# Strassen operands from normalized rows, and six pools in the down stage, in a one-core hybrid encoder layer

## The chip, the cores and the metric

The kernel runs on one core of one Trainium2 chip. The metric is device time in microseconds (us), median of several runs. Engines go by their short names in the profile: PE is TensorE, DVE VectorE, ACT ScalarE, POOL GpSimd, SP SyncE (here it only starts DMAs).

## The reference, cut to what matters

One encoder layer (DEPTH is 1) is applied to two sequences of 512 rows with 1024 columns each, all in float32:

```
h = _rmsnorm(x, norm_mix_g[l])
...
x = x + (g_a * y_a + g_b * y_b) @ w_out[l]
h = _rmsnorm(x, norm_ffn_g[l])
gt, up = jnp.split(h @ w_gu[l], 2, axis=-1)
x = x + (jax.nn.silu(gt) * up) @ w_down[l]
...
return _rmsnorm(x, final_norm_g)
```

y_a is a bidirectional RWKV7 branch, y_b an attention branch. The change is in the last part: the norm ahead of the feed-forward, the product with w_gu (1024 x 5632) and the product with w_down (2816 x 1024). `_rmsnorm` divides each row by the root of its mean square and multiplies each column by a gain.

## The kernel before, in words

**Precision.** A float32 operand is split into two rounded parts, `hi` (a cast on ACT) and `lo = x - hi` (a subtraction on DVE or POOL). One product is three matmuls: hi x hi, hi x lo, lo x hi (`mm3`, L139). `split` (L135) makes the pair; all matmuls are recorded at L129, all transposes at L133 (`tr4`, four 128 x 128 blocks into one PSUM bank).

**Stages.** First the branches (to about 900 us), then `combine` of each sequence (products with w_oab, tile `pab`), the projections with w_out (`pwo`, added to the residual rows `x2`), then the feed-forward and the final norm.

**Strassen.** The feed-forward treats the two sequences together: seven block products instead of eight. With the normalized, transposed rows of sequence 0 in column halves B11 and B21 and those of sequence 1 in B12 and B22, the operands are B11, B21, B22, T1 = B12 - B11, T2 = B22 - T1, T3 = B22 - B12 and T4 = B21 - T2, each as hi and lo, of 128 x 4 x 512. B12 itself isn't kept. The weights get the matching sums S1 to S4, formed on POOL per block of 128 feed-forward columns (`a_blocks`, L1332).

**First norms** (`first_norm`, L1280): called for the four tiles of sequence 0 from inside `combine` of sequence 1, at steps 0, 2, 4 and 6 of its eight. Squares on ACT, a power on POOL, a row scaling on DVE (L1292), per half a group of four transposes (`nt_f0`), a column scaling by the gain from PSUM on DVE (L1296), the cast on ACT and the `lo` part on POOL (`EF`).

**The planned window** (L1423 to L1550). `Window` is a small planner: operations with an engine, a cost, a rank and dependences; it writes their order out ahead, and the instructions of each engine are kept in that order. It holds the last quarter of the projections (`w_project`), the norms of sequence 1 (`w_norm`), T1 to T4 (`w_norm` forms T1, B22, T2 and T3, `w_combos` T4 and the splits into memory that is free only once the projection's weights are gone, `reopen`), and the first four products of the feed-forward (`w_product`, blocks 0 and 1 with B11 and B21). There the rows of sequence 1 are scaled (L1462), transposed (two groups per tile), scaled by the gain (L1471), and everything else works on transposed data: T1 takes two subtractions (L1479, L1481), the others one or two, on POOL or DVE as the strings ET1 to ET4 and EB22 say.

**Feed-forward, first half** (`gate_up`, L1368): 22 blocks; `pgA`, `pgB` and `pgC` are its PSUM tiles. Weights come in as `graw` and `uraw` of 512 KB through three buffers (`raw`, NRAW). Results go to DRAM (`a_d`).

**Down stage** (from L1574): again seven products, over eleven pairs of blocks, two at a time (`turns`). Once the operands' pools are closed (`tp_` for T2 to T4, `evst` for the evaluation tiles, `bst` for B11, B21, B22, T1 and the products kept), one pool `fp` takes all tiles: ten halves `rh` of loaded data, eleven each of `w12`, `t` and `s` that stay resident, seven pairs of split blocks `d`, and the tiles of the ends. `p5_(0)` copies W12 from the raw tile of block 0 (L1665) and forms the first T from that copy (L1671).

All these DMAs are issued by SP, whose queue is served in order: a load that waits for its buffer holds those behind it.

Of the kernel before, what the change touches and what calls it, by code (L numbers as in the profile page):

```python
# [18 lines left out]
P = 128  # L19
# [56 lines left out]
ET2 = 'gggg'  # L76
# [3 lines left out]
C0 = 14  # L80
HK = (0, 2, 4, 6)
# [13 lines left out]
EB22 = 'gggg'  # L95
ET1 = 'ggvv'
ET3 = 'gggg'
ET4 = 'vggg'
ES = 'gg'
EF = 'gggg'  # L100
# [8 lines left out]
def trunk(ctx, tc, outs, x, w_in, w2, g2, w_uq, w_ukk, w_ukv, w_oab, w_out, w_gu, w_down,  # L109
          cols, fng, ident, te, to, mask2, reset, blk64, blk2):  # L110
# [1167 lines left out]
    B11, B21 = (operand(bp0, n) for n in ("B11", "B21"))  # L1278

    def first_norm(cp_, t):  # L1280
# [10 lines left out]
        for g, dst in enumerate((B11, B21)):  # L1291
            nc.vector.tensor_scalar_mul(h[g], xs[:, g], ss[:, 0:1])  # L1292
# [131 lines left out]
    COST = {nc.vector: ("V", 0.6), nc.gpsimd: ("G", 1.23)}  # L1424
    early, psb = {}, []

    def w_split(dst, t, src, rank, eng, *deps):
        ts = slice(t * P, (t + 1) * P)
        hi = W.op("A", 0.52, rank, lambda: nc.scalar.copy(dst()[0][:, :, ts], src()), *deps)
        lo = W.op(*COST[eng], rank, lambda: eng.tensor_sub(dst()[1][:, :, ts], src(), dst()[0][:, :, ts]), hi)  # L1430
        return hi, lo

    def w_project(t):
# [3 lines left out]
        def mms(k0):  # L1437
            if k0 == 0:
                z["ps"] = bank(1 + t % 2, f"pwo1{t}")
# [4 lines left out]
        o = psb[-4:-3]  # L1444
# [5 lines left out]
    def w_norm(t, old):  # L1450

        ts, xt, z = slice(t * P, (t + 1) * P), x2[4 + t], {}

        def square():
            z["ss"] = np_.tile([P, 1], F32, tag="nss", bufs=4, name=f"nssf1{t}")
            z["ht"] = np_.tile([P, D], F32, tag="nh", bufs=1, name=f"nhf1{t}")
            return nc.scalar.activation(z["ht"], xt, AF.Square, accum_out=z["ss"])
        o = W.op("A", 1.04, 0, square, *psb[-1:], *old.get("tr", ()))
        o = W.op("V", 0.07, 0, lambda: nc.vector.tensor_scalar(z["ss"], z["ss"], 1.0 / D, RMS_EPS,
                                                               op0=ALU.mult, op1=ALU.add), o)  # L1460
        o = W.op("G", 0.46, 0, lambda: nc.gpsimd.tensor_tensor(z["ss"], z["ss"], mhalf[:, :1], op=ALU.pow), o)
        o = W.op("V", 0.66, 0, lambda: nc.vector.tensor_scalar_mul(z["ht"], xt, z["ss"]), o)  # L1462
        r = {"tr": [], "nsc": [], "z": z}

        def tr(g):
            z["ps", g] = bank(3, f"nt_f1{t}{g}")
            tr4(z["ps", g], lambda i: z["ht"][:, (g * 4 + i) * P:(g * 4 + i + 1) * P])

        def scale(g):
            z[g] = np_.tile([P, KH, P], F32, tag=f"nsc{g}", bufs=(4, 1)[g], name=f"nscf1{t}{g}")  # L1470
            return nc.vector.tensor_mul(z[g], z["ps", g].rearrange("p (k t) -> p k t", k=KH),  # L1471
                                        cc(C_GFFN + g * KH, KH).unsqueeze(2).to_broadcast([P, KH, P]))
        for g in range(2):
            r["tr"].append(W.op("T", 0.43, 0, lambda g=g: tr(g), o, *old.get("nsc", [])[g:g + 1]))
            r["nsc"].append(W.op("V", 0.6, 0, lambda g=g: scale(g), r["tr"][g], *(old.get("b22", ()) if g else ())))
# [31 lines left out]
    def w_product(i):  # L1507
# [20 lines left out]
        for k in range(KH):  # L1528
            o = [W.op("T", 0.64, 3 + i, lambda k=k: mms(k), *o)]
# [321 lines left out]
```

## Time and profile before

| What | us |
|---|---|
| median of 3 runs | 1795.2 (1794.31 to 1796.43) |
| the profiled execution | 1793.97 |
| its span, first to last instruction | 1792.2 |
| PE busy | 1700.9 (95%) |
| DVE busy | 1075.6 (60%) |
| ACT busy | 787.9 (44%) |
| POOL busy | 627.3 (35%) |

The mean granted TensorE clock is 0.984. A row of the profile gives a line of the kernel, an engine, an operation and `out<-in` by the program's tile names with numbers left out; `x` is a count. In the table by stage each engine's busy time is followed by its number of instructions; PEclk is the granted clock as a share of full speed. Matmuls overlap in the pipeline, so one of them is reported longer (389 ns) than the step from one to the next, and a busy PE is not PE at its peak.

### The profile page before, as it was taken

The page shows a single profiled execution, that of the slowest core. Times are in us where ns is not written, and L with a number is a line of the kernel's source. Part 1 is how long each engine was busy: PE and PEld are TensorE (multiplying, and loading weights), DVE is VectorE, ACT ScalarE, POOL GpSimd, SP SyncE. Part 2 cuts the span into 40 slices and gives each one's busy share as a digit, 9 for nine tenths or more (in the row PEclk, how much of TensorE's full clock was granted, in tenths as well). Part 3 has the DMA queues.
Part 4 walks back from the last instruction along what each step waited for, and adds up shares of the span by engine and source line. Part 5 has one row for each costly group of instructions (what it writes and reads, how often), then busy time and mean ns, then how long its engine had stood idle before and what let it go on. Part 6 is the DMA issues. An engine that isn't in the chain of part 4 may idle for free.

```text
span 1792.2 us, 30028 instructions
## 1 busy us (share of the span) xinstructions
PE 1700.9 (95%) x11276; PEld 1327.8 (74%) x11276; DVE 1075.6 (60%) x1773; ACT 787.9 (44%) x1533; POOL 627.3 (35%) x984
## 2 busy tenths in 40 slices
PE   7999999999999997999999999699999999989997
PEld 6778766777777775666667877488888888868886
DVE  6734464636445365855566665955565465498657
ACT  6643424344433335666663432433333333245445
POOL 1121536274554736261012143833343333200006
PEclk9999999999999998999999999899999999999999
DMA  5473342434334344211267531123222222383442
GB/s 179 135 259 100 107 116 79 132 86 125 114 85 121 84 116 118 73 40 34 110 207 266 176 126 36 36 88 107 94 93 96 83 90 76 100 307 110 130 134 94
DMA packets 181233, 208.90 MB, mean 117 GB/s; under 512 B 102816, under 2 KB 106272, under 8 KB 181088
## 3 DMA queue, kind: packets, MB, share of 16 engines
q1 hardware_dynamic: 180224, 205.48, 36.3%
q8 instruction: 88, 1.44, 0.3%
q10 hardware_dynamic: 720, 0.98, 0.2%
q0 software_dynamic: 144, 0.52, 0.1%
q14 instruction: 57, 0.47, 0.1%
HBM read 147.70 MB, written 59.24 MB: 115 GB/s over the span
## 4 chain that ended last, share of the span: by engine, by line
PE 72%; DVE 9%; POOL 6%; DMA 6%; issue 3%; ACT 2%; SPq 1%; DVEq 0%; POOLq 0%; ACTq 0%
PE pgC L129 10%; PE pj_gt L129 8%; PE pgB L129 6%; PE pgA L129 6%; PE pj_rkv L129 4%; PE dx L129 4%; PE pwo L129 4%; PE pab L129 3%; PE s L129 2%; PE dy L129 2%; POOL el L966 2%; POOL lt L964 2%; PE sc L129 2%; PE pj_mla L129 2%; PE pav L129 2%
## 5 line engine op out<-in xcount | busy, mean ns | idle before, releaser
L964 POOL TENSOR_TENSOR lt<-lane,el 128x126 f32<-128x126 f32 (+22 forms) x248 | 94.1, 379 | 36.7 <-DMA lane<-nt_d 18.1
L966 POOL TENSOR_TENSOR el<-el,lt 128x126 f32<-128x126 f32 (+22 forms) x248 | 98.9, 399 | 19.0
L129 PE MATMUL pab<-yo,wab 128*128 128x512 f32 x384 | 96.5, 403 | 5.5 <-DVE wab L137 2.8
L129 PE MATMUL pj_gt<-h_hi,wlo_gt 128*128 128x512 f32 x240 | 98.4, 410 | 1.2 <-DVE wlo_gt L137 1.2
L129 PE MATMUL pj_gt<-h_lo,whi_gt 128*128 128x512 f32 x240 | 99.4, 414 | 0.0
L129 PE MATMUL pj_gt<-h_hi,whi_gt 128*128 128x512 f32 x240 | 99.0, 412 | 0.0
L129 PEld LDWEIGHTS pab<-yo,wab 128*128 128x128 f32 x384 | 71.7, 191 | 24.2 <-DVE wab L137 5.1
L1344 POOL TENSOR_TENSOR s<-uraw 128x512 f32<-128x512 f32 x22 | 29.3, 1334 | 154.3 <-DMA uraw<-in_w_gu 154.0
L129 PE MATMUL pwo<-woh,m 128*128 128x512 f32 x256 | 80.4, 390 | 0.0
L129 PE MATMUL pj_rkv<-h_hi,wlo_rkv 128*128 128x512 f32 x192 | 79.1, 412 | 0.0
L129 PE MATMUL pj_rkv<-h_hi,whi_rkv 128*128 128x512 f32 x192 | 78.6, 410 | 0.0
L129 PE MATMUL pj_rkv<-h_lo,whi_rkv 128*128 128x512 f32 x192 | 78.2, 407 | 0.0
L1720 POOL TENSOR_TENSOR x<-x,dp 128x512 f32<-128x512 f32 x4 | 6.3, 1593 | 177.5 <-DVE x L1719 177.5
L1412 DVE TENSOR_TENSOR p<-p,pgC 128x512 f32<-128x512 f32 x22 | 15.1, 687 | 82.3 <-PE pgC L129 82.3
L1053 ACT COPY sva<-s 64x128 f32<-64x128 f32 x64 | 16.5, 258 | 100.8 <-PE s L129 87.3
L129 PEld LDWEIGHTS pwo<-woh,m 128*128 128x128 f32 x256 | 48.1, 188 | 10.0
L1054 DVE COPY svb<-s 64x128 f32<-64x128 f32 x64 | 18.9, 295 | 60.5 <-ACT sva L1053 35.8
L775 DVE TENSOR_REDUCE mx<-sc 128x1 f32<-128x512 f32 x64 | 43.6, 687 | 15.7 <-PE sc L129 14.9
L129 PEld LDWEIGHTS pj_gt<-h_hi,wlo_gt 128*128 128x128 f32 x240 | 45.1, 188 | 9.9 <-DVE wlo_gt L137 1.7
L129 PEld LDWEIGHTS pj_gt<-h_hi,whi_gt 128*128 128x128 f32 x240 | 45.1, 188 | 8.9
L129 PEld LDWEIGHTS pj_gt<-h_lo,whi_gt 128*128 128x128 f32 x240 | 45.1, 188 | 8.6
L1354 POOL TENSOR_TENSOR s<-graw,uraw 128x512 f32<-128x512 f32 x22 | 29.2, 1325 | 63.8 <-DVE S_2l L137 5.0
(1563 smaller groups left out, 5458.4 us busy)
## 6 DMA issues: line engine op xcount, KB each, us to landing
graw<-in_w_gu SPq DMA_DIRECT2D x22, 512.0 KB, 3.6
uraw<-in_w_gu SPq DMA_DIRECT2D x22, 512.0 KB, 3.6
a_d<-a SPq DMA_DIRECT2D x21, 512.0 KB, 3.4
w<-in_w_down SPq DMA_DIRECT2D x42, 256.0 KB, 4.5
x<-in_x SPq DMA_DIRECT2D x16, 512.0 KB, 7.1
rwkv_in<-lut SPq DMA_DIRECT2D x32, 256.0 KB, 2.4
gate_d<-gtt SPq DMA_DIRECT2D x32, 256.0 KB, 2.4
wab<-in_w_oab SPq DMA_DIRECT2D x32, 256.0 KB, 3.8
```

The lines of the kernel that those rows point to most:

```text
L129: pin(nc.tensor.matmul(out, lhsT, rhs, start=start, stop=stop, **kw), n if out.shape[0] > 64 else n / 2)
L775: nc.vector.tensor_reduce(mx, sc, axis=AX.X, op=ALU.min)
L964: eng.tensor_mul(lv, lane[:, s, s + 1:].unsqueeze(1).to_broadcast([P, m_, n]), el[:, 0:m_, s].unsqueeze(2).to_broadcast([P, m_, n]))
L966: eng.tensor_add(ev, ev, lv)
L1053: nc.scalar.copy(sva[HA, :, c], s2[HA])
L1054: nc.vector.tensor_copy(svb[HB, :, c], s2[HB])
L1344: vg(ES[min(j, 1)]).tensor_add(s1, a21, a22)
L1354: vg(ES[min(j, 1)]).tensor_sub(s3, a11, a21)
L1412: nc.vector.tensor_add(p1, p1, x_)
L1720: nc.gpsimd.tensor_add(xs(1, t, 1), xs(1, t, 1), p5[t])
```

## The change

In `first_norm` the gain is multiplied into the rows before they are transposed: it comes as a tile `gain` of 128 x 1024 (`ffg`, the gain repeated on all partitions) that takes one of the three `raw` buffers. The normalized rows go to DRAM as well (`n0_d`, eight stores of 256 KB). The split reads PSUM directly, its `lo` part on DVE.

In the window, the rows of sequence 1 get the gain in the same way; the rows of sequence 0 are fetched again (`w_row`); T1, T3, T2 and T4 are formed on rows, on DVE, with one subtraction each; and T1, B22, T2, T3 and T4 are each transposed (`w_tr`: five groups of four per tile) and split from PSUM, `hi` on ACT and `lo` on DVE. The strings that put work on POOL go away. The projections of the window use one PSUM bank pair instead of two; ranks and costs of the planner are new (R1, R2, RW, RP).

In the down stage `fp` becomes six pools: `frh` (the `rh` halves), `fs`, `ft`, `fp` (ends), `fd` (split blocks) and `fw12`. The first copy of W12 moves to POOL, and the first T reads the raw tile.

```diff
@@ first_norm
         for g, dst in enumerate((B11, B21)):
-            nc.vector.tensor_scalar_mul(h[g], xs[:, g], ss[:, 0:1])
+            nc.vector.scalar_tensor_tensor(out=h[g], in0=xs[:, g], scalar=ss[:, 0:1], in1=gain[:, g * S:(g + 1) * S],
+                                           op0=ALU.mult, op1=ALU.mult)
+            nc.sync.dma_start(n0_d[t][:, g], h[g])
             ps = dn(f"nt_f0{t}{g}")
             tr4(ps, lambda i: h[g][:, i * P:(i + 1) * P])
-            sc = ld(f"nscf0{g}").rearrange("p (k t) -> p k t", k=KH)
-            nc.vector.tensor_mul(sc, ps.rearrange("p (k t) -> p k t", k=KH),
-                                 cc(C_GFFN + g * KH, KH).unsqueeze(2).to_broadcast([P, KH, P]))
-            split(dst[0][:, :, ts], dst[1][:, :, ts], sc, vg(EF[t]))
+            split(dst[0][:, :, ts], dst[1][:, :, ts], ps.rearrange("p (k t) -> p k t", k=KH))
@@ the window
+    def w_tr(t, name, i, src, dst, rank, late, *deps):
...
+        def tr():
+            z["ps"] = bank(i, f"nt_{name}{t}")
+            tr4(z["ps"], lambda c: src()[:, c * P:(c + 1) * P])
+            z["v"] = z["ps"].rearrange("p (k t) -> p k t", k=KH)
+        o = W.op("T", 0.44, rank, tr, *deps, *late, *[r[0] for r in trs[i][-1:]], *[r[1] for r in trs[i][-2:-1]])
+        hi = W.op("A", 0.6, rank, lambda: nc.scalar.copy(dst()[0][:, :, ts], z["v"]), o)
+        lo = W.op("V", 0.68, rank, lambda: nc.vector.tensor_sub(dst()[1][:, :, ts], z["v"], dst()[0][:, :, ts]), hi)
...
+    def w_row(t, g, rank, *deps):
...
+            z["w"] = np_.tile([P, S], F32, tag="w", bufs=2, name=f"n0{t}{g}")
+            return nc.sync.dma_start(z["w"], n0_d[t][:, g])
...
+        na = W.op("V", 0.7, 0, lambda: scale(0), o)
+        w, ld = w_row(t, 0, 0)
+        t1 = W.op("V", 0.7, 0, lambda: nc.vector.tensor_sub(w["w"], z["n"][:, 0], w["w"]), na, ld)
+        o1, _ = w_tr(t, "T1", 3, lambda: w["w"], lambda: T1, 0, (), t1)
+        nb = W.op("V", 0.7, R1[0], lambda: scale(1), o)
+        b22, _ = w_tr(t, "B22", 2, lambda: z["n"][:, 1], lambda: B22, R1[1], (), nb)
+        t3 = W.op("V", 0.7, R1[2], lambda: nc.vector.tensor_sub(z["n"][:, 0], z["n"][:, 1], z["n"][:, 0]), nb, t1)
+        t2 = W.op("V", 0.7, R1[2], lambda: nc.vector.tensor_sub(z["n"][:, 1], z["n"][:, 1], w["w"]), t3, b22, o1)
...
+    def w_third(t, z, t3, t2):
+        w_tr(t, "T3", 2, lambda: z["n"][:, 0], lambda: T3, R2[1] + t, (opened,), t3)
+        w, ld = w_row(t, 1, R2[2])
+        o = W.op("V", 0.7, R2[2] + t, lambda: nc.vector.tensor_sub(w["w"], w["w"], z["n"][:, 1]), ld, t2)
+        wbuf.append(w_tr(t, "T4", 3, lambda: w["w"], lambda: T4, R2[2] + t, (opened,), o)[0])
@@ the down stage
-    fp = pool(p4, "fp")
+    frh, fs, ft, fp, fd, fw12 = (pool(p4, n) for n in ("frh", "fs", "ft", "fp", "fd", "fw12"))
...
         if p == 0:
-            nc.vector.tensor_copy(W12[p], pre["draw"][0][:, hihalf])
+            nc.gpsimd.tensor_copy(W12[p], pre["draw"][0][:, hihalf])
...
-        nc.vector.tensor_sub(T_[p], W12[p], w11)
+        nc.vector.tensor_sub(T_[p], W12[p] if p else pre["draw"][0][:, hihalf], w11)
```

More of the change, by code (lines that the diff above doesn't have):

```diff
@@ L80 @@
 C0 = 14
+R1, R2, RW, RP = (1, 1, 2), (3, 10, 14), 1, 3
 HK = (0, 2, 4, 6)
@@ L1278, in trunk @@
     B11, B21 = (operand(bp0, n) for n in ("B11", "B21"))
+    n0_d = [dram.tile([P, 2, S], F32, name=f"n0_d{t}") for t in range(4)]
+    gain = fwr[0].tile([P, D], F32, tag="raw", bufs=NRAW, name="ffg")
+    nc.sync.dma_start(gain, ffg)
     def first_norm(cp_, t):
@@ L1438, in mms @@
             if k0 == 0:
-                z["ps"] = bank(1 + t % 2, f"pwo1{t}")
+                z["ps"] = bank(1, f"pwo1{t}")
             hi, lo = wo1[k0 // 2]
@@ L1448, in w_project @@
         return o[0]
[L1450 to L1459, printed above, removed]
-                                                               op0=ALU.mult, op1=ALU.add), o)
[L1461 to L1467, printed above, removed]
-        def scale(g):
[L1470 to L1475, printed above, removed]
-        def t1():
-            z["t1"] = np_.tile([P, KH, P], F32, tag="nt", bufs=3, name=f"ntf{t}")
-            return nc.vector.tensor_sub(z["t1"], z[0], B11[0][:, :, ts])
-        a = W.op("V", 0.6, 0, t1, r["nsc"][0], *(n[-3].get("T4", ()) if t > 2 else ()))
-        o = W.op("V", 0.6, 0, lambda: nc.vector.tensor_sub(z["t1"], z["t1"], B11[1][:, :, ts]), a)
-        r["T1"] = w_split(lambda: T1, t, lambda: z["t1"], 0, vg(ET1[t]), o)
-        b = w_split(lambda: B22, t, lambda: z[1], PRIOW, vg(EB22[t]), r["nsc"][1])
-        eng = vg(ET3[t])
-        d = W.op(*COST[eng], PRIOW, lambda: eng.tensor_sub(z[0], z[1], z[0]), r["nsc"][1], a)
-        eng2 = vg(ET2[t])
-        r["T2"] = W.op(*COST[eng2], PRIOW, lambda: eng2.tensor_sub(z["t1"], z[1], z["t1"]), *r["T1"], r["nsc"][1])
-        r["b22"], r["T3"] = (*b, d, r["T2"]), d
-        return r
@@ L1491, in w_combos @@
[L1491 to L1498 removed]
+    trs = {2: [], 3: []}
@@ L1535, in w_product @@
             copied.append(W.op("A", 0.48, 1, copy, *o, *copied[-1:]))
-    n, last, copied = [{}], [], []
+    n, last, copied = [], [], []
     fw = T2 = T3 = T4 = None
@@ L1541, in trunk @@
         last.append(w_project(t))
-        if t == 3:
-            opened = W.op(None, 0, 0, reopen, *last)
-            for i in range(3):
-                w_combos(i, n[i + 1])
-        n.append(w_norm(t, n[-1]))
-    w_combos(3, n[4])
+        n.append(w_norm(t))
+    opened = W.op(None, 0, 0, reopen, *last)
+    for f in (w_second, w_third):
+        for t in range(4):
+            f(t, *n[t])
     for i in range(2 * NE):
@@ L1582, in d_half, with resident @@
     def d_half(src, name):
-        raw = fp.tile([P, 512], F32, tag="rh", bufs=NRH, name=name)
+        raw = frh.tile([P, 512], F32, tag="rh", bufs=NRH, name=name)
         nc.sync.dma_start(raw, src)
         return raw
-    def resident(tag, name):
-        return fp.tile([P, 512], F32, tag=tag, bufs=JP, name=name)
+    def resident(pl, name):
+        return pl.tile([P, 512], F32, tag="r", bufs=JP, name=name)
     def d_block(src, name):
         cnt[0] += 1
-        pl, tag, bufs = (fw, "b", NBLK) if cnt[0] % 2 else (fp, "d", DBLK)
+        pl, tag, bufs = (fw, "b", NBLK) if cnt[0] % 2 else (fd, "d", DBLK)
         hi = pl.tile([P, 512], F32R, tag=f"{tag}hi", bufs=bufs, name=f"{name}h")
@@ L1813, in layout @@
     r["fng"] = np.broadcast_to(a["final_norm_g"], (P, D)).copy()
+    r["ffg"] = np.broadcast_to(a["norm_ffn_g"][0], (P, D)).copy()
     r["ident"] = np.eye(P, dtype=f)
```

60 lines of the change are left out of this document (33 added, 27 removed).

## Prediction

> **What bounds the kernel now.** I read the page's head first, then a table by stage (busy time per engine between chosen times), because the share of TensorE is an average over stages with different limits.
>
> ```profile
> span 1792.2 us, 30028 instructions
> ```
> ```profile
> core 0: us, PE busy (x) PEld busy (x) DVE busy (x) ACT busy (x) POOL busy (x), PEclk, DMA share, GB/s
> 1017.00:1063.50 46.50, 43.03 (x192) 33.97 (x192) 38.48 (x59) 20.81 (x43) 22.05 (x18) 0.96 0.42 136
> 1093.10:1117.60 24.50, 22.60 (x107) 18.28 (x105) 14.26 (x21) 7.47 (x13) 11.17 (x10) 1.00 0.00 0
> 1093.10:1167.20 74.10, 55.90 (x237) 44.13 (x236) 57.08 (x61) 28.42 (x51) 51.66 (x36) 0.88 0.07 22
> 1200.00:1550.00 350.00, 350.00 (x1546) 289.82 (x1545) 196.78 (x247) 118.96 (x203) 128.45 (x91) 1.00 0.28 91
> 1558.80:1612.60 53.80, 44.98 (x194) 35.59 (x192) 45.64 (x75) 19.75 (x35) 0.77 (x1) 1.00 0.71 254
> 1612.60:1770.00 157.40, 157.36 (x694) 130.31 (x695) 117.29 (x181) 79.22 (x148) 22.28 (x16) 1.00 0.36 111
> ```
>
> The row 1200 to 1550 is TensorE without a gap: 350 / 1546 = 0.226 us from one matmul to the next. That is the yardstick. The row after 1612 is dense too (0.227), so whatever is won before it moves the end by as much. The other rows are where the change acts, and each loses time:
> - first norms (1017 to 1063.5): 32 of the 192 are transposes, which cost 0.45 per four (row below). 160 x 0.226 + 8 x 0.45 = 39.8, so 6.7 of 46.5 is lost.
> - the planned window (1093.1 to 1167.2; last projection, second norms, Strassen operands, first products): 205 x 0.226 + 8 x 0.45 = 49.9, so 24.2 of 74.1 is lost.
> - start of the down stage (1558.8 to 1612.6): 194 x 0.226 = 43.8, so 10.0 of 53.8 is lost.
>
> Next, who makes TensorE wait in the window (the view of waits), and the groups of that stretch (the view of lines):
>
> ```profile
> PE nt_f L133 <- DVE nhf L1462: 6.6, 3, 4.7
> PE pgB L129 <- ACT T L1429: 5.9, 1, 5.9
> PE pgB L129 <- DVE T L1430: 3.7, 1, 3.7
> ```
> ```profile
> L1430 DVE TENSOR_TENSOR T<-ntf,T 128x512 fp32r<-128x512 f32 x10 | 13.1, 1330 | 0.0
> L1485 POOL TENSOR_TENSOR nscf<-nscf,nscf 128x512 f32<-128x512 f32 x4 | 6.9, 1735 | 6.3 <-ACT B L1429 3.9 <-DVE ntf L1479 2.3
> L1462 DVE TENSOR_SCALAR nhf<-x,nssf 128x1024 f32<-128x1024 f32 x4 | 6.0, 1510 | 4.8 <-POOL nssf L1461 4.8
> L1471 DVE TENSOR_TENSOR nscf<-nt_f,col 128x512 f32<-128x512 f32 x8 | 5.2, 683 | 2.1 <-PE nt_f L133 2.1
> L129 PE MATMUL pgB<-T,S_0h 128*128 128x512 f32 x8 | 4.3, 607 | 9.6 <-ACT T L1429 5.9 <-DVE T L1430 3.7
> L1344 POOL TENSOR_TENSOR s<-uraw 128x512 f32<-128x512 f32 x3 | 4.8, 1599 | 1.1 <-DMA uraw<-in_w_gu 0.8 <-PE pwo L129 0.3
> L1447 DVE TENSOR_TENSOR x<-x,pwo 128x512 f32<-128x512 f32 x4 | 2.7, 679 | 2.9 <-PE pwo L129 2.9
> ```
>
> Compare two rows of one shape: a VectorE operation takes 683 ns when one operand lies in PSUM (L1471; 679 in L1447), and 1330 ns on average when all its operands lie in SBUF (L1430), in a stretch in which GpSimd is busy 51.66 of 74.1. So VectorE and GpSimd are the bound of this stretch, partly by holding each other up; the waits named give 16.2 of the 24.2, and the rest is a slow clock after them (granted 0.88; 607 ns for a matmul of pgB).
>
> **Part 1, the window.** *Removed:* all operand work of GpSimd (the splits of B22, the differences T3 and T2, two splits of T1 and three tiles' T4: 20 operations, at up to 1.735 us, the L1485 row), and on VectorE the whole-row scaling (L1462), two column scalings and the second subtraction of T1. *Added:* differences are formed on normalized rows, so five things per tile are transposed instead of two: 12 more groups of four transposes.
>
> ```profile
> 1102.81 0.45 PE nt_f L133 x4
> ```
>
> 12 x 0.45 = 5.4 more on TensorE, all of it on the path, since the stretch is to become TensorE's. VectorE per tile: the projection's add, two scalings by row and gain, T1, T3, T2, the T4 difference and five splits, so 12 operations; 48 x 0.68 = 32.6. Nine more splits of weight blocks: 6.1. Together 38.7. It can start with the first add, 24 x 0.226 = 5.4 after 1093.1, and end at 1137.2. TensorE has 96 projection matmuls, 20 groups of transposes and 48 early products: 144 x 0.226 + 20 x 0.45 = 41.5, to 1134.6. So the two are nearly level and VectorE is 2.6 behind. GpSimd keeps about seven sums of weight blocks (L1344 and its neighbours); each can hold a VectorE operation for 1.60 - 0.68 = 0.92 if both its operands are in SBUF, 6.4 at most. The five splits now read PSUM, which the 683 ns row shows undisturbed. What is last, T4 (8 of the 48 operations), is used only four products, 48 x 0.226 = 10.8 us, later. So the loss that stays lies between 0 and 2.6 + 6.4 = 9.0, and I take 6, nearer the upper end since the order is fixed ahead and every slip stops TensorE in order. **Gain 24.2 - 5.4 - 6 = 12.8**, from 9.8 to 18.8 by these bounds.
>
> A new wait comes with it. The gain's tile takes one of the three `raw` buffers until the last row scaling, so the second half of block 0 (`uraw0`), long in memory before, is loaded after that.
>
> ```profile
> uraw<-in_w_gu SPq DMA_DIRECT2D x22, 512.0 KB, 3.6
> w<-in_w_down SPq DMA_DIRECT2D x42, 256.0 KB, 4.5
> rwkv_in<-lut SPq DMA_DIRECT2D x32, 256.0 KB, 2.4
> ```
>
> The last projection ends at 1093.1 + 96 x 0.226 + 6 x 0.45 = 1117.5; add, squares, power, two scalings behind it I put at 5 us (estimate: some seven steps of 0.68). Load from 1122.5 to 1126.1, one sum of 1.60, and a split of 2 x 0.68: S1 at 1129, before TensorE is through with its 41.5. So it costs nothing while those 1134.6 cover it, and shows in full past them. Rows of the first half are stored and fetched again (256 KB, 2.4 to 4.5 us each, eight out and eight in); the fetch for T1 has no producer nearby and is hidden, the one for T4 waits for a free buffer but has 10.8 us. Projections now use one bank pair instead of two: each is freed by a 0.68 add, two tiles (10.8 us) before it is wanted again; nothing.
>
> **Part 2, first norms.**
>
> ```profile
> 1042.84 2.75 DVE L1292 TENSOR_SCALAR nhf<-x,nssf 128x512 f32<-128x512 f32 x2
> ```
> ```profile
> 1042.61 2.69 POOL L137 TENSOR_TENSOR B<-nscf,B 128x512 fp32r<-128x512 f32 x2
> ```
> ```profile
> 1046.84 4.60 PE L129 MATMUL pab<-yo,wab 128*128 128x512 f32 x12 [2.57 <-DVE wab L137]
> ```
> ```profile
> 1038.61 3.53 DMA g<-gate_d
> ```
>
> One of the losses is seen whole here: two row scalings (2.75 us) stand as long as GpSimd splits B (2.69), the weight split behind them is late, TensorE waits 2.57. The change takes these eight GpSimd splits away, drops eight column scalings on VectorE (8 x 0.68) and puts eight splits there instead, which is level; the row scaling takes the gain with it, at 0.68 each. Two at 0.68 against 2.75 leave 1.4 per tile. Against it: SyncE now also issues eight stores of 256 KB, each of which waits for its scaled rows, and the loads of gates and weights behind them wait too (one such load, 3.53, is on the chain of waits already). Bounds: +5 (all losses but 1.7 gone) to -7 (two loads made late); I take a **gain of 2**.
>
> **Part 3, start of the down stage.** The chain of waits, and SyncE's own waits:
>
> ```profile
> 1553.62 2.72 PE pgB L129 x12
> ...
> 1562.68 2.73 PE pgC L129 x12
> ...
> 1566.16 0.69 DVE a L1413
> 1566.85 0.35 DVE w L1665
> ...
> 1567.23 0.70 DVE T L1671
> ...
> 1568.01 0.32 SPq L1323
> ```
> ```profile
> SPq L1323 <- DVE T L1671: 13.4, 1, 13.4
> ```
> ```profile
> PE dy L129 <- ACT dS_0h L136: 3.5, 1, 3.5
> ```
>
> Nothing of the pool `fp` is done on VectorE until the last use of the feed-forward's evaluation tiles (L1413); then W12's copy and the first difference T. The load of the third `araw` waits 13.4 us for that difference, and every load behind it in SyncE's queue with it; then the DMA share jumps to 0.71 over the stretch while TensorE starves. Operand memory itself falls free in turn: B11 and B21 before B22 and T1, those before the evaluation tiles, T4 last at 1562.68 + 2.73 = 1565.4. Six pools in that order let `rh`, S and T start once B22's products are done (1553.62 + 2.72 = 1556.3), nine us earlier, and the first T no longer waits for W12's copy. W12 goes to the memory that is freed last: its first load from 1565.4 lands at 1569.9, the difference and split take 3 x 0.68, 1572.0. TensorE has eight matmuls of its first products left behind T4's, to 1567.2, and two products of 12 x 0.226 before it needs them, at 1572.6. Just enough. The copy on GpSimd hides (first use a phase later), but holds one `raw` buffer some 1.5 us longer (estimate from 1.60 for a sum of that shape). The split of T for the first product needs T4's memory too: 2 x 0.68 after 1565.4, at about 1566.8. I take 2.5 of the 10.0 as staying: **gain 7.5**, bounds 0 and 10.
>
> **Sum.** 12.8 + 2 + 7.5 = 22.3. The profiled execution took 1793.97 (span 1792.2 and 1.8 around it); 1793.97 - 22.3 = 1771.7. The median of the runs is 1.2 above that execution, so 1773 against 1795.2.
>
> **Rivals.**
> - *The pools change nothing* (VectorE's order is fixed by something other than memory, or W12's late loads stop SyncE's queue as the third `araw` did). For: W12 is now on the latest memory. Against: 13.4 us for one load that needs only T. 1773 + 7.5 = 1780.5.
> - *`uraw0` comes late.* If its issue stands in SyncE's queue behind the T4 fetches, which wait for T4 transposes at about 1140 (estimate: VectorE's 1137.2 and a few slips), S1 is ready at 1140 + 3.6 + 1.6 + 1.4 = 1146.6 instead of being hidden to 1134.6; other products can't go ahead, as they all need that load. 12 more, of which 2 lie in my 6: 1773 + 10 = 1783.
> - *The clock falls.* In this row transposes follow an idle stretch and the clock is slow after it:
>
> ```profile
> 1127.49 1.94 PE L133 MATMUL nt_f<-idn,nhf 128*128 128x128 f32 x8 [4.68 <-DVE nhf L1462]
> ```
>
> After 1117.5 TensorE has 14 groups of transposes and 48 matmuls, with VectorE pacing; at half speed these 17.2 us cost 17 more: 1790. Against it: 1093.1 to 1117.6 holds 24 transposes at a granted 1.00, though between projections. The Trainium skill, "TensorE: Matmul & The Clock Gate", Part 4: PE-mode transpose, says that a transpose "doesn't count as PE-busy the same way", which speaks against this change; no stretch of transposes alone is in this trace to test it.
> - *Slower: SyncE's queue in the first norms.* Eight stores wait for their scalings ahead of loads that feed the products at once. One late load costs one landing, 3.53. If more than six of eight do (22.3 / 3.53), all is lost; with all eight, 28.2 - 22.3 = 5.9 slower: 1801. Against it: one such wait is seen in the stretch today, and there are four tiles spread over eight steps.
> - *All waits vanish:* 6 + 2.5 + 3 more gained: 1761.5.
>
> **Chances.** Forecast 0.52 (its own range 1766 to 1780), pools without effect 0.13, late `uraw0` 0.14, clock 0.07, stores 0.10, all vanish 0.04. About 0.2% (3.6 us) is what a measurement of this kernel can tell from no change; the clock's 1790 lies 1.6 beyond that, so half of its chance goes to no change. Faster 0.86, same 0.04, slower 0.10. The range 1763 to 1788 takes in the forecast, the late load, the pools, and parts of the others: 0.84.
>
> **What would show it.** Right: between the last projection and the feed-forward's first products GpSimd has only weight sums and powers; T's VectorE splits take near 0.68; no wait of TensorE in the window above 3 us; five transposed things per tile; the third `araw` load issued before 1565 less the gain so far; dy's first product right behind dx. Wrong: TensorE waiting for S1's split with GpSimd's sum waiting for `uraw` (late load), a granted clock under 0.9 after the projections with TensorE busy (clock), pab waiting for wab or g with SyncE waiting for the scaled rows (stores), or SyncE waiting for T4's last product with loads for `rh` behind it (pools).

## The result, and the profile after

The changed kernel takes 1775.63 us (median of 4 runs, 1774.83 to 1783.75), the kernel before 1795.82, measured beside it (4 runs): a ratio of 0.9897 with a 95% interval of 0.9867 to 0.9928, 13 to 24 us less. A second series with more runs gave 1775.44 against 1792.49, ratio 0.9902 (0.9884 to 0.9920). The profiled execution took 1774.83 us (span 1773.0). The forecast was 1773.0, with a range of 1763 to 1788.

The first view is the table by stage of the changed kernel; its rows stand against those of the prediction (line numbers of the changed kernel are about five lower up to `first_norm` and eight to ten higher in the down stage). Columns: stretch, its length, then each engine's busy time with its instructions, granted clock, DMA share, GB/s.

```profile
1014.00:1060.00 46.00, 44.90 (x208) 35.69 (x208) 34.19 (x62) 21.77 (x44) 12.31 (x10) 1.00 0.58 189
1089.00:1160.00 71.00, 69.05 (x339) 55.88 (x338) 55.72 (x84) 32.85 (x64) 22.43 (x18) 1.00 0.19 60
1200.00:1530.00 330.00, 330.00 (x1458) 273.25 (x1457) 184.22 (x232) 112.56 (x192) 120.02 (x86) 1.00 0.27 91
1540.00:1600.00 60.00, 56.69 (x237) 45.06 (x236) 54.63 (x90) 23.88 (x42) 1.49 (x2) 0.97 0.70 243
1600.00:1750.00 150.00, 150.00 (x647) 121.62 (x646) 107.76 (x165) 74.30 (x140) 21.88 (x16) 1.00 0.33 107
```

Read with the prediction's prices (0.226 a matmul, 0.45 for four transposes):
- First norms: 208 less 32 transposes are 176 x 0.226 + 8 x 0.45 = 43.4, so 2.6 of 46.0 is lost, against 6.7 before: 4.1 gained.
- Window: 259 x 0.226 + 20 x 0.45 = 67.5, so 3.5 of 71.0 is lost, against 24.2. Less the 5.4 for twelve more groups of transposes, 15.3 is gained. The granted clock is 1.00 and GpSimd is busy 22.43 of 71 in place of 51.66 of 74.
- Gate and up stage: 330 / 1458 = 0.2263, as before.
- The last row is the surprise: no gap, clock 1.00, and yet 150 / 647 = 0.2318 a matmul, where the kernel before had 157.4 / 694 = 0.2268. (The step from the start of one matmul to the start of the next is called the pitch from here on.)

Two rows of the window carry its mechanism: VectorE's splits from PSUM take 681 ns each, where the splits of T took 1330 on average before (L1430 there), and the longest wait of TensorE that is left is 0.9 us, where it was 5.9.

```profile
L1452 DVE TENSOR_TENSOR T<-nt_T,T 128x512 fp32r<-128x512 f32 x16 | 10.5, 681 | 0.3 <-ACT T L1451 0.2
```
```profile
PE pgB L124 <- ACT S_1h L131: 0.9, 1, 0.9
```

The timeline of TensorE shows where the time went in total: the first matmul of the `pwo` stage, the first of the down stage and the last one, in the changed kernel and then in the kernel before.

```profile
973.72 0.39 PE L124 MATMUL pwo<-woh,m 128*128 128x512 f32 x1
...
1539.88 0.39 PE L124 MATMUL dx<-P1drawh,P1arawh 128*128 128x512 f32 x1
...
1764.68 0.40 PE L124 MATMUL dx<-dT_10h,dA_10l 128*128 128x512 f32 x1
```
```profile
973.52 0.39 PE L129 MATMUL pwo<-woh,m 128*128 128x512 f32 x1
...
1558.89 0.39 PE L129 MATMUL dx<-P1drawh,P1arawh 128*128 128x512 f32 x1
...
1783.97 0.39 PE L129 MATMUL dx<-dT_10h,dA_10l 128*128 128x512 f32 x1
```

Up to the down stage 585.4 became 566.2, which is 19.2 less. The down stage itself, of which the prediction hoped for 7.5, takes 224.8 after 225.1. Its start did become better: the first S begins just before the first down product, the copy of W12 stands on GpSimd, and of four larger waits (3.5 us for `dS_0h`, which the prediction shows, and the three of the first view) one is left (the second view). After them the timelines of DVE, POOL and SP and the chain of waits, all of the changed kernel:

```profile
PE dx L129 <- ACT dA_4h L136: 2.3, 1, 2.3
PE dx L129 <- ACT dA_3h L136: 1.5, 1, 1.5
PE dy L129 <- DVE dT_1l L137: 1.1, 1, 1.1
```
```profile
PE dx L124 <- ACT dA_3h L131: 2.7, 1, 2.7
```
```profile
1539.68 0.69 DVE L1678 TENSOR_TENSOR S<-araw,a 128x512 f32<-128x512 f32 x1 [1.63 <-DMA a<-a_d]
1540.29 1.10 DVE L1679 TENSOR_TENSOR T<-draw 128x512 f32<-128x512 f32 x1
```
```profile
1540.11 0.73 POOL L1673 COPY w<-draw 128x512 f32<-128x512 f32 x1 [8.71 <-PE pgC L124]
```
```profile
1545.78 0.32 SPq L1320 DMA_DIRECT2D araw<-a_d  x1
1546.19 2.28 SPq L1675 DMA_DIRECT2D w<-in_w_down  x5
1548.58 0.36 SPq L1320 DMA_DIRECT2D araw<-a_d  x1
...
```
```profile
1548.58 8.10 DMA araw<-a_d
...
1556.78 0.63 ACT dA_3h L131
...
1557.45 2.08 PE dx L124 x4
1559.53 2.51 PE dy L124 x8
```

The load that the prediction watched, the third `araw`, goes out at 1545.78, before the first dy product. The next one goes out 2.8 us later, behind five loads of W12 on the same queue, and takes 8.10 us, in which the DMA engines are busy 0.95 of the time; TensorE waits 2.7 for it and then runs slow (four matmuls in 2.08, eight in 2.51, at a granted clock of 0.66 from 1557 to 1562). By the row 1540 to 1600, 237 x 0.226 = 53.6, so 6.4 of 60 is lost against 10.0: 3.6 gained. The slower pitch behind it gives as much back: some 700 matmuls from 1600 on at 0.005 more are 3.5.

### The profile page after: what moved, and what is told of

The parts are those of the page before. It is cut to its first block, busy times and chain, and to the rows that moved or that the text cites. A ratio compares the mean times of both kernels' runs of the same rounds, so it can differ in the third digit from the quotient of the medians.

```text
span 1773.0 us, 30134 instructions
## 1 busy us (share of the span) xinstructions
PE 1705.7 (96%) x11324; PEld 1329.0 (75%) x11324; DVE 1060.9 (60%) x1784; ACT 787.8 (44%) x1541; POOL 584.8 (33%) x957
## 4 chain that ended last, share of the span: by engine, by line
PE 71%; DMA 8%; POOL 7%; DVE 7%; issue 3%; ACT 3%; SPq 1%; DVEq 0%; POOLq 0%; ACTq 0%
PE pgC L124 10%; PE pj_gt L124 8%; PE pgB L124 7%; PE pgA L124 6%; PE dx L124 5%; PE pwo L124 4%; PE dy L124 3%; PE pj_rkv L124 3%; PE s L124 3%; POOL el L961 2%; POOL lt L959 2%; PE pab L124 2%; PE sc L124 2%; PE pav L124 2%; PE pj_mla L124 2%
## 5 line engine op out<-in xcount | busy, mean ns | idle before, releaser
L770 DVE TENSOR_REDUCE mx<-sc 128x1 f32<-128x512 f32 x64 | 43.7, 687 | 15.6 <-PE sc L124 14.8
L1177 POOL TENSOR_TENSOR g<-g 128x512 f32<-128x512 f32 x16 | 24.9, 1555 | 84.7 <-DVE g L1175 66.7
```

The costliest lines, as they stand in the source:

```text
L770: nc.vector.tensor_reduce(mx, sc, axis=AX.X, op=ALU.min)
L1177: nc.gpsimd.tensor_add(g_[:, 0], g_[:, 0], g_[:, 1])
```

## The experiments

The question is what made the same matmuls slower, then what the parts are worth, and what the two new waits cost. My first theory came from the layout of the built program. A matmul has a stationary operand (128 x 128), which is loaded ahead of it (PEld in the profile), and a moving one (128 x 512). In the down stage, its first product apart, the moving operand lies in `fd` (`fp` before) and the stationary one in `fw`. `fw` starts at byte 190,432 of each partition, 224 modulo 256 (the remainder after division by 256). So did the moving blocks before (138,464). In the changed kernel `fd` starts at 134,496, 96 modulo 256, because pool `fp` now lies below it and ends in two small tiles, `fss` and `frs`, 128 bytes together. In the gate and up stage everything starts at 224.

Two spans stand beside each median: from the first `pwo` matmul to the first down matmul (up), and from there to the last down matmul (down), both from the profiled execution; then the matmuls in the 45 us from 1640 to 1685.

| run | median us | ratio to before (95%) | up | down | matmuls |
|---|---|---|---|---|---|
| before | 1795.82 | | 585.4 | 225.1 | 200 |
| after | 1775.63 | 0.9897 (0.9867, 0.9928) | 566.2 | 224.8 | 195 |
| after_again | 1775.44 | 0.9902 (0.9884, 0.9920) | 566.3 | 224.9 | 195 |
| a_align224 | 1769.19 | 0.9870 (0.9848, 0.9892) | 566.4 | 221.0 | 200 |
| b_shift128 | 1797.87 | 1.0028 (1.0016, 1.0040) | 585.8 | 230.4 | 194 |
| early_only | 1776.98 | 0.9914 (0.9883, 0.9944) | 566.8 | 228.5 | 200 |
| down_only | 1794.13 | 0.9997 (0.9985, 1.0010) | 585.7 | 226.2 | 195 |
| one_pool | 1773.53 | 0.9889 (0.9860, 0.9918) | 565.9 | 224.0 | 200 |
| no_gain | 1772.67 | 0.9881 (0.9861, 0.9901) | 567.7 | 221.5 | 200 |
| no_stores | 1769.41 | 0.9866 (0.9844, 0.9888) | 564.8 | 222.8 | 200 |
| araw_far | 1768.51 | 0.9859 (0.9837, 0.9881) | 566.4 | 219.3 | 200 |
| best | 1768.41 | 0.9863 (0.9842, 0.9885) | 567.9 | 218.1 | 200 |
| m_offsets, one run | 1781.59 | | 575.6 | 221.7 | 196 |
| m_fine, one run | 1780.53 | | 566.6 | 225.8 | 197 |

The experiments were made in four series, and each ratio is against the kernel before of its own series: 1792.86 (`a_align224`, `b_shift128`, `early_only`, `down_only`), 1793.23 (`m_offsets`, `no_gain`, `no_stores`, `araw_far`), 1793.55 (`m_fine`, `one_pool`) and 1792.49 (`best`, `after_again`). The last series ran on another chip than the first three. Where kernels share the up part its span agrees within 0.9 us (565.9 to 566.8); the medians scatter more, since the stages ahead of `pwo` alone moved its start between 968.0 and 978.1.

### Does the place of the small tiles set the pitch?

`a_align224` changes only this in the changed kernel:

```diff
-    frh, fs, ft, fp, fd, fw12 = (pool(p4, n) for n in ("frh", "fs", "ft", "fp", "fd", "fw12"))
+    frh, fs, ft, fp, fd, fw12, fsm = (pool(p4, n) for n in ("frh", "fs", "ft", "fp", "fd", "fw12", "fsm"))
...
-        ss = fp.tile([P, 2], F32, tag="fss", ...
-        rs = fp.tile([P, 1], F32, tag="frs", ...
+        ss = fsm.tile([P, 2], F32, tag="fss", ...
+        rs = fsm.tile([P, 1], F32, tag="frs", ...
```

> The changed kernel with the two small tiles of the last norms (fss and frs, 2 x 64 B a partition) in a pool of their own behind the last one, so that the down stage's moving operands, the fd blocks, start 128 B lower: at 224 modulo 256 bytes, as the kernel before has them and as every operand of the gate and up stage lies, in place of 96 modulo 256. Nothing else moves. Theory (the start address of the moving operand sets the pitch of the matmuls): the down stage goes back from 0.232 to 0.225-0.227 us a matmul between 1600 and 1750, and the time falls by 3.5 to 5 us against the changed kernel, to about 1771 us. Rival (the slower pitch comes from the pools' other traffic, from the loads that land earlier or from the weights' tiles): the pitch stays at 0.232 and the time at 1775.

`b_shift128` does the reverse to the kernel before, in `p5_`:

```diff
         S_[p] = resident("s", f"S{p}")
+        if p == 0:
+            pad = fp.tile([P, 32], F32, tag="pad", bufs=1, name="pad")
+            nc.gpsimd.memset(pad, 0.0)
```

> The kernel before with a pad of 128 B (one tile, cleared once by GpSimd) put ahead of the moving operands of the down stage in its one pool: they start at 96 modulo 256 in place of 224, and nothing else of the change is in it. Theory (start address): the pitch of the down stage rises from 0.2245-0.2265 to 0.232 us a matmul and the time by 3.5 to 5 us, to 1799-1801 us. Rival (pools, loads): pitch and time stay, 1796 us.

The same 45 us of the down stage by stage table: first the changed kernel, then `a_align224`, then `b_shift128`.

```profile
1640.00:1685.00 45.00, 45.00 (x195) 36.49 (x194) 29.84 (x48) 19.27 (x35) 0.00 (x0) 1.00 0.39 124
```
```profile
1640.00:1685.00 45.00, 45.00 (x200) 37.28 (x199) 30.98 (x50) 19.62 (x36) 0.00 (x0) 1.00 0.41 129
```
```profile
1640.00:1685.00 45.00, 45.00 (x194) 36.21 (x193) 30.71 (x50) 19.17 (x34) 0.00 (x0) 1.00 0.32 102
```

In all three TensorE has no gap and the granted clock is 1.00; 195, 200 and 194 matmuls fit. 128 bytes ahead of the moving blocks make the whole difference, in both directions. The down stage falls by 3.8 us in `a_align224` and rises by 5.3 in `b_shift128`. The start of the stage differs in its waits and, for `b_shift128`, in its granted clock (0.91 over the first 60 us), so the fair stretch lies behind it: from the first matmul of `dy<-dT_7h,dS_7h` to the last of the stage, at a clock of 1.00 in all four, the kernel before takes 169.4 us, `a_align224` 170.0, and the changed kernel and `b_shift128` 173.4 each. So the address is worth 3.4 to 4.0 us there. The medians agree less sharply: `b_shift128` is 5.0 above the kernel before of its series; `a_align224` is 23.7 below its own, the changed kernel 20.2 and 17.1 in its two series. The rival, that loads or pools slow the matmuls, is out: `b_shift128` has neither.

### The address alone, or where the two operands stand to each other?

`m_offsets` gives every buffer of both operands a start address of its own (`d_block`; the stationary blocks likewise through a helper with five buffers):

```diff
-        hi = pl.tile([P, 512], F32R, tag=f"{tag}hi", bufs=bufs, name=f"{name}h")
-        lo = pl.tile([P, 512], F32R, tag=f"{tag}lo", bufs=bufs, name=f"{name}l")
...
+            i = (cnt[0] // 2 - 1) % DBLK
+            hi = fd.tile([P, 512], F32R, tag=f"dhi{i}", bufs=1, name=f"{name}{'abcdefg'[i]}h")
+            lo = fd.tile([P, 520 if i != 5 else 528], F32R, tag=f"dlo{i}", bufs=1, ...)
+            lo = lo[:, :512]
```

> The changed kernel, small tiles in a pool of their own, with the buffers of the down stage's matmul operands placed at different start addresses: the seven pairs of moving blocks at 224, 0, 32, 64, 96, 128 and 192 modulo 256 bytes, the five pairs of stationary blocks (also those of the gate and up stage) at 224, 0, 32, 64 and 96. The pitch of each block's twelve matmuls is read from the timeline by buffer. Theory (the moving operand's own start address counts): 0.227 us for moving blocks at 224 whatever the stationary block, 0.233 at 96, and another value for each class of the other five; the gate and up stage, where all moving operands stand at 224, keeps 0.2264 for all five stationary offsets. Rival (what counts is where moving and stationary operand stand to each other): the pitch goes with the difference of the two offsets, a moving block at 224 slows down beside a stationary one at 96, and the gate and up stage slows down for some of its five.

The letters in the names tell the buffers. The timeline below has the first and last matmul of two neighbouring blocks of twelve: `gl`/`yl` has the moving block at 192 and the stationary one at 96, `al`/`ul` has both at 224.

```profile
1635.91 0.40 PE L124 MATMUL dx<-dT_4gh,dS_4yh 128*128 128x512 f32 x1
...
1638.49 0.39 PE L124 MATMUL dx<-dT_4gh,dS_4yl 128*128 128x512 f32 x1
1638.72 0.40 PE L124 MATMUL dy<-dB_3ah,dS_3uh 128*128 128x512 f32 x1
...
1641.22 0.40 PE L124 MATMUL dy<-dB_3ah,dS_3ul 128*128 128x512 f32 x1
```

2.58 / 11 = 0.2345 in the one and 2.50 / 11 = 0.2273 in the other, side by side. The mean step in ns between starts within a block, over the whole down stage (some twenty steps each, from times printed to 10 ns, so a few tenths of a nanosecond mean nothing; steps outside 218 to 245, at waits, left out), by moving offset (rows) and stationary offset (columns):

| | 224 | 0 | 32 | 64 | 96 |
|---|---|---|---|---|---|
| 224 | **226.8** | 232.7 | 233.1 | 234.0 | 232.8 |
| 0 | 233.2 | **229.1** | 233.3 | 232.3 | 234.1 |
| 32 | **230.0** | 233.3 | **229.1** | 232.8 | 233.1 |
| 64 | 233.8 | **229.1** | 233.3 | **228.6** | 232.8 |
| 96 | 233.3 | 233.3 | **228.6** | 232.8 | **229.1** |
| 128 | 233.6 | 233.9 | 235.0 | **228.2** | 233.3 |
| 192 | 233.3 | 233.6 | 233.0 | 233.3 | 234.5 |

My theory falls here: no offset of the moving block is fast or slow by itself. The rival holds: fast are the pairs at the same place modulo 256 (the diagonal) and those where the moving block stands 64 bytes ahead; all the others take 232 to 235. The gate and up stage says the same, with all moving operands at 224: 227.6 for stationary blocks at 224 and 232.5 to 233.9 for the four others, which cost this kernel 9 us. The period isn't longer than 256: by the layout of the built program of `a_align224`, the gate and up stage has pairs at a distance of 0 modulo 512 and others at 256, and both take 226.8. The row of that stage in `m_offsets` and then in `a_align224`, in the view of TensorE alone:

```profile
1180.00:1540.00 360.00, 360.00 (x1553) 1.00 0.27 89
```
```profile
1180.00:1540.00 360.00, 360.00 (x1590) 1.00 0.29 97
```

`m_fine` has all stationary blocks at 224 and takes slices of the moving ones at finer distances:

```diff
...
+            o = (0, 2, 4, 12, 16, 20, 60)[i]
+            hi, lo = (fd.tile([P, 576], F32R, tag=f"d{n}{i}", bufs=1, ...)[:, o:o + 512]
+                      for n in "hl")
```

> As the kernel with varied offsets, but all stationary blocks (and all buffers) start at 224 modulo 256, and the seven pairs of moving blocks of the down stage are slices that begin 0, 8, 16, 48, 64, 80 and 240 bytes behind that. The run before this one gave 227 to 230 ns a matmul where the moving block stood 0 or 64 B ahead of the stationary one modulo 256 and 232 to 235 for the other six distances in steps of 32 B. Theory (a relation between the two addresses alone): 0 and 64 give 227 to 229; the distances between belong to one class or the other with nothing in between, and none is below 226. Rival (the best distance lies between the steps of 32 B): one of 8, 16, 48, 80 or 240 falls below 224 ns. If the distance didn't matter, but something else that differed by buffer: seven equal values.

| distance, bytes | 0 | 8 | 16 | 48 | 64 | 80 | 240 |
|---|---|---|---|---|---|---|---|
| ns a matmul | 226.9 | 234.5 | 231.8 | 230.3 | 228.8 | 230.0 | 233.6 |

None is below 226, so equal places are the best seen, and the kernel before had them. "Nothing in between" was wrong: 16, 48 and 80 give values between the classes. The runs show the relation, not its cause: a weight load (PEld, 188 ns) runs beside each matmul, but what collides was not measured.

### What the parts are worth

`early_only` is the changed kernel up to the gate and up stage with the down stage of the kernel before; `down_only` the reverse.

> The changed kernel up to the gate and up stage, and the down stage of the kernel before (one pool, W12 copied on VectorE). By the two traces (the first down product 19.0 us earlier, the down stage itself 233.0 us in both) this part alone gives the whole gain: 1776.5 us, 19 below the kernel before. By the prediction's terms it gives 14.8, 1780.5 us.

> The kernel before up to the gate and up stage, and the down stage of the changed one (six pools, W12 copied on GpSimd). By the two traces: the waits at the start of the stage shrink by 3.7 us and the slower pitch takes as much, so 1795.5 us, no change that can be measured. By the prediction's term: 7.5 us faster, 1788 us. If a pool's layout were of no use: 1796 us with the first down waits of the kernel before still there.

`down_only` came out as the traces had said: no change (ratio 0.9997). `early_only` took the 1776.98 us that they had said, but the kernel before was faster in this series (1792.86), so it is only 15.9 us below it, with an interval of 10 to 21 that holds both forecasts, 19 and 14.8. What decides is its span up to the down stage, 18.6 us shorter than before (585.4 to 566.8), and `down_only`. So the whole gain is that of the window and the first norms, and the down stage's edits are worth nothing net, where the prediction had 7.5. They are worth nothing because one effect eats the other. The down spans of four runs make a square: with one pool 225.1 at equal places (kernel before) and 230.4 shifted (`b_shift128`), with six pools and the copy on GpSimd 221.0 (`a_align224`) and 224.8 (changed kernel). The edits bring 4.1 to 5.6 us at either address, and the shift takes 3.8 to 5.3. By the medians they bring 7.8 us against `early_only` (1776.98 to 1769.19), though the intervals of the two ratios overlap.

`one_pool` splits that: `early_only` with the two small edits,

```diff
-            nc.vector.tensor_copy(W12[p], pre["draw"][0][:, hihalf])
+            nc.gpsimd.tensor_copy(W12[p], pre["draw"][0][:, hihalf])
...
-        nc.vector.tensor_sub(T_[p], W12[p], w11)
+        nc.vector.tensor_sub(T_[p], W12[p] if p else pre["draw"][0][:, hihalf], w11)
```

> The changed kernel with the one pool of the kernel before in the down stage (its moving blocks are at 224 modulo 256 in it), but W12's first copy on GpSimd and the first T formed of the raw block, as changed. Theory (the waits of the down stage's start hang on when the one pool's memory comes free): the down stage from its first to its last matmul takes as long as with one pool and no edit, within 1 us of 228.5, against 221.0 with six pools at the same alignment. Rival (the copy on VectorE was what the first sums stood behind): 222 to 225.

Waits of TensorE from 1535 to 1600 in `one_pool` and in `a_align224`:

```profile
PE dy L124 <- ACT dS_0h L131: 3.3, 1, 3.3
PE dx L124 <- ACT dA_3h L131: 2.1, 1, 2.1
PE dx L124 <- ACT dA_5h L131: 1.3, 1, 1.3
```
```profile
PE dx L124 <- ACT dA_3h L131: 3.0, 1, 3.0
PE dx L124 <- ACT dA_4h L131: 0.3, 1, 0.3
PE dx L124 <- ACT dA_9h L131: 0.3, 1, 0.3
```

The wait for `dS_0h`, the first S, is what the pools take away: with one pool VectorE begins it at 1547.95, 10.1 us after the first down matmul, with six at 1537.83, 0.2 before it. The size is less sure. The down span is 228.5 in `early_only`, 224.0 in `one_pool` and 221.0 in `a_align224`, so the copy edit has a share too, as the rival said. But part of the 228.5 is a lower granted clock in that one profile (0.89 from 1534 to 1580 and 0.91 over the last 18 us, where the same code had 1.00 in the kernel before and took 225.1). Against that 225.1 the copy brings 1.1 and the pools 3.0, each from one profile, and neighbouring intervals of the ratios overlap. The split between pools and copy stays open.

### What is left: the fourth activation block

`araw_far` gives the third block 4 KB of its own, so that the fourth gets the raw buffer that the third had waited for, ahead of the W12 loads:

```diff
+            if p == 2:
+                araw[p] = far.tile([P, D], F32, tag="r", bufs=1, name="araw2")
+                nc.sync.dma_start(araw[p], a_d[p].rearrange("p b s -> p (b s)"))
+            else:
...
```

> The changed kernel, small tiles in a pool of their own, and the third activation block of the down stage (araw2) in 4 KB of its own in place of the third turn of the raw buffers: its load waits for T4's memory alone, and the load of araw3 takes the raw buffer that becomes free at 1543.9 us, ahead of the five W12 loads that it stood behind. Theory (what is left of the down stage's waits, 3.0 us for dA_3h and the lower granted clock after it, comes from that queue): the wait goes, 2.5 to 4.5 us faster, 1765 to 1766.7 us. Rival (the transfers are at the memory's limit there, near 400 GB/s, so another block is late in its place): 1768 to 1770.

The wait for `dA_3h` goes, and another comes (waits of TensorE, then the chain of waits):

```profile
PE dy L124 <- DVE dT_1l L132: 1.9, 1, 1.9
```
```profile
1548.89 5.77 DMA w<-in_w_down
```

Now the first of the W12 loads is behind the activations, and the product that needs it waits 1.9. The down span falls by 1.7 (221.0 to 219.3); the median, 1768.51, is in the rival's range and can't be told from the 1769.19 of `a_align224`. Both were half right: the queue's order was the wait's cause, and where the transfers run at 342 to 371 GB/s (1550 to 1570, 0.97 to 1.00 of the DMA engines' time) they partly only change places.

### The late raw buffer

`no_gain` scales the window's rows without the gain (this part of the computation is left out), so the gain's tile gives its raw buffer back after the first norms.

```diff
-            return nc.vector.scalar_tensor_tensor(out=z["n"][:, g], in0=xt[:, g], scalar=z["ss"][:, 0:1],
-                                                  in1=gain[:, g * S:(g + 1) * S], op0=ALU.mult, op1=ALU.mult)
+            return nc.vector.tensor_scalar_mul(z["n"][:, g], xt[:, g], z["ss"][:, 0:1])
```

> The changed kernel, small tiles in a pool of their own, with the second batch's rows of the window scaled without the gain (this part of the computation is left out): the gain's tile, which holds one of the three raw buffers up to 1118.75 us in the changed kernel, is free when the first norms end, so that the load of uraw0 doesn't wait for the window. Theory (the late raw buffer costs only what TensorE waits for S_0 and S_1, 1.6 us in all): faster by 0.5 to 2 us than the same kernel with the gain (1769.2). Rival (the chain of raw buffers sets the pace of the early products, as the prediction's rival had it with 4.5 us and more): faster by 4 us or more.

Neither: the up part takes 1.3 us more (567.7). GpSimd's and VectorE's timeline of `no_gain`, then the same VectorE operations (L1495, L1479, L1486) in `a_align224`:

```profile
1114.27 1.28 POOL L1341 TENSOR_TENSOR s<-uraw 128x512 f32<-128x512 f32 x1 [3.77 <-PE pwo L124]
1115.63 1.64 POOL L1342 TENSOR_TENSOR s<-s,graw 128x512 f32<-128x512 f32 x1
```
```profile
1114.83 1.28 DVE L1494 TENSOR_TENSOR n<-n,n 128x512 f32<-128x512 f32 x1
1116.03 1.25 DVE L1479 TENSOR_TENSOR nssf<-nssf 128x1 f32<-128x1 f32 x1
...
1118.51 1.50 DVE L1486 TENSOR_SCALAR n<-x,nssf 128x512 f32<-128x512 f32 x1 [0.44 <-POOL nssf L1482]
```
```profile
1112.53 0.68 DVE L1495 TENSOR_TENSOR n<-n,n 128x512 f32<-128x512 f32 x1
1113.40 0.16 DVE L1479 TENSOR_TENSOR nssf<-nssf 128x1 f32<-128x1 f32 x1 [0.19 <-ACT n L1476]
...
1114.79 0.75 DVE L1486 SCALAR_TENSOR_TENSOR n<-x,nssf,ffg 128x512 f32<-128x512 f32 x1 [0.44 <-POOL nssf L1482]
```

With `uraw0` in memory early, GpSimd forms S1 and S2 at 1114 to 1117, in the middle of VectorE's last norm, and an addition of one column takes 1.25 in place of 0.16: it ends at 1117.28, GpSimd's second sum at 1117.27. The chain that TensorE waits for is made longer by more than the two S waits (1.6) were worth; TensorE waits 1.6 for a T1 that is late. The Trainium skill, "SBUF — State Buffer", section "SBUF: two separate sides", has a GpSimd operation that reads SBUF and a VectorE operation with two inputs in SBUF hold a shared pair of ports one at a time, the other blocked; these rows agree (0.16 against 1.25). The late load which the prediction listed as a danger keeps GpSimd out of VectorE's way, and costs nothing net here. (1.3 us is little more than the 0.9 by which equal up parts differ; the stretched rows are what carries this reading.)

### The eight stores on SyncE

`no_stores` leaves the stores of the first norms' rows out and lets the window fetch rows of x (other data in T1 and T4; that part of the computation is changed).

```diff
-            nc.sync.dma_start(n0_d[t][:, g], h[g])
...
-            return nc.sync.dma_start(z["w"], n0_d[t][:, g])
+            return nc.sync.dma_start(z["w"], x[0][t * P:(t + 1) * P, g * S:(g + 1) * S])
```

> The changed kernel, small tiles in a pool of their own, without the eight stores of the first norms' rows; the window loads rows of x in their place (so its T1 and T4 are formed of other rows). Theory (the stores are hidden: SyncE's queue has room, and what the first norms gained came from the chain without the scaled copy): time and first norms as with the stores, 1769 within 1 us. Rival (the stores hold up the weights behind them on SyncE): the first norms' stretch loses 1 to 2.6 us less, 1766.5 to 1768.

The stretch 1010 to 1060 in `a_align224` and in `no_stores`:

```profile
1010.00:1060.00 50.00, 48.76 (x225) 38.87 (x224) 35.97 (x64) 22.37 (x45) 12.33 (x10) 1.00 0.56 180
```
```profile
1010.00:1060.00 50.00, 49.99 (x232) 40.16 (x232) 36.23 (x65) 23.12 (x47) 12.32 (x10) 1.00 0.46 147
```

Without the stores TensorE has no gap left in this stretch (the wait for `wab`, 1.1 us, is gone), and the up part is 1.6 us shorter (564.8), more than the 0.9 by which equal up parts differ. So the stores cost some 1 to 1.6 us, by the mechanism of the prediction's slower rival at a small fraction of its price, against what I expected here. The whole time doesn't tell (1769.41 against 1769.19): the down stage, whose code is the same, took 1.8 more in this profile, at 0.91 over its last 18 us.

### Together

`best` is `araw_far` with the stores issued by GpSimd (`nc.gpsimd.dma_start`); `after_again` is the changed kernel.

> The changed kernel with three things that the runs so far point to: the small tiles in a pool of their own (moving and stationary blocks of the down stage at the same place modulo 256 bytes), the third activation block in 4 KB of its own, and the eight stores of the first norms' rows issued by GpSimd in place of SyncE. Theory (the three add up: 4 to 5 us, 1.7 us and 1.1 to 1.6 us in their stages): about 7 us below the changed kernel of the same call, 1767 us where that is 1774. Rival (GpSimd's stores hold up its own pow and gate operations in the first norms, so that stretch loses what SyncE gains): 5.5 us below, or less.

> The changed kernel itself once more, on the chip of the experiments, so that they can be set against it in times of one call. Expected: 18 to 19 us below the kernel before, 1774 to 1776 us, and between 1600 and 1740 us 604 matmuls against 620 with the operands at the same place modulo 256.

1768.41 against 1775.44, 7.0 us less. The spans say that the rival is right about the stores: the down stage gives 6.7 (224.9 to 218.1) and the up part takes back 1.6 (566.3 to 567.9). Some of the 6.7 is the clock: the same down stage took 219.3 in `araw_far`, at 0.97 over its first 60 us where `best` had 1.00. The stores wait for their rows in GpSimd's queue (waits of POOL from 1010 to 1060), where the gate operations stand behind them, and TensorE waits 2.1 for weights where it had waited 1.1:

```profile
POOL n_d L1292 <- DVE nhf L1290: 5.4, 4, 2.1
```
```profile
PE pab L124 <- DVE wab L132: 2.1, 2, 1.5
```

`araw_far`, with the stores left on SyncE, has the smallest sum of both spans (785.6; `best` 786.0, the changed kernel 791.0), half a microsecond that decides nothing against `best`, and the same median as `best` within the runs' scatter.

## Why the prediction was right, and which of its steps were not

The time came out 2.6 us from the forecast, but as a sum of terms that were off in both directions. The mechanism of the two early parts was right; that the sum came so close is luck, since what the window and the first norms gave beyond the forecast (4.6) made up for most of what the down stage fell short (7.2).

- **Window, 12.8 predicted, 15.3 found.** The traces bear out the mechanism: the price of transposes held (from the start of a group to the second matmul behind it 0.67, which less one step of 0.226 leaves 0.44 for the group), GpSimd's operand work is gone, no wait of TensorE in the stretch exceeds 0.9 us. The term that was mis-sized is the loss that stays, 6 reserved near the upper bound of 9, 3.5 found. VectorE's splits from PSUM ran undisturbed (681 ns). No run takes the window apart: the planner's new ranks and the single bank pair came with the row form, and their share is not shown.
- **First norms, 2 predicted, 4.1 found.** With GpSimd's splits gone, VectorE's row scalings, now with the gain, take 0.75 each in place of 1.23, near the 0.68 of the prediction, and the wait for `wab` falls from 2.6 to 1.1. This outweighs the stores, which cost up to 1.6 (`no_stores`); no run has the shorter chain alone.
- **Down stage, 7.5 predicted, 0.3 found.** Two steps failed. "I take 2.5 of the 10.0 as staying": 6.4 stayed (6.2 by the same count in `a_align224`, where the slower pitch plays no part). The prediction followed the third `araw` and the first W12 load, which came as it said; the next `araw` was behind five W12 loads that the new pools had set free together. And "the row after 1612 is dense too (0.227), so whatever is won before it moves the end by as much": the pitch of a dense stretch was taken as fixed, but the edit moved the operands' addresses, and 0.2268 became 0.2318. With the addresses mended the down stage falls by 4.1 against the kernel before (225.1 to 221.0).
- **Sum.** Predicted 22.3; found 19.1 between the two profiled executions: the two early terms gave 4.6 more than forecast, the down stage 7.2 less (the stages' rounded prices leave 0.6 unassigned).
- **Rivals.** *Pools change nothing*: so it came out for the down stage, and its second reason points at something real: W12's loads do stand on SyncE ahead of a block of activations. But the queue isn't stopped, as that reason had it: SyncE's wait for T4's last product there is 0.2 us; the block goes out 2.8 later by the five issues ahead of it, and what the pools did win went to the pitch, which no rival had. *Late `uraw0`*: it came late, about as the prediction's own timing had it and not as late as the rival's, and cost nothing net (`no_gain`). *Clock*: 1.00 in the window with 80 transposes among 339 instructions. The Trainium skill's sentence on transposes ("TensorE: Matmul & The Clock Gate", Part 4: PE-mode transpose) had no effect here; as the transposes lie between matmuls, 12 in a row at most (1132.4 to 1135.4), a longer stretch of transposes alone remains untested. *Stores*: real, up to 1.6 us instead of 28.

## What to carry to other kernels

Look at the operands' addresses whenever pools are rearranged: a dense stretch has a pitch of its own, and here a small tile ahead of a pool of blocks cost some 5 ns on every matmul behind it; put small tiles behind the large ones, or start both operands at the same place modulo 256 bytes. Compare matmuls per stretch between two traces even where TensorE shows no gap. And when memory is freed earlier, ask which loads will now go out together and which of them is needed first.

## What was not expected of the hardware

- The step between these matmuls (fp32r, 128 x 128 by 128 x 512) depends on where the moving and the stationary operand stand to each other modulo 256 bytes: 227 to 230 ns at a distance of 0 or 64, 232 to 235 at every other multiple of 32, 234.5 at 8. The Trainium skill, "SBUF — State Buffer", section "A bandwidth-pool intuition that's wrong (but worth ruling out)", gives weight loads a read port of their own, independent of the moving operand's. A port of its own gives no reason for the distance to matter; the measurement shows that it does, by 2 to 3%, and the measurement decides.
- The price of a wait isn't its length: the granted clock fell after some waits and not after others. The same down stage took 225.1 us in one profile at 1.00 and 228.5 in another at 0.89 over its start. At its end the waits were the same in both (1.5 and 0.7 us, 1.5 and 0.6), and 71 matmuls fitted into 18.4 us at 1.00 and 64 at 0.91.
- GpSimd's sums stretched a VectorE addition of a single column from 0.16 to 1.25 us, so that a load that came earlier made the stage longer.
